# Attention's results stored by halves of the tokens, four heads in a buffer

## The chip, the cores and the metric

The kernel runs on one NeuronCore of one Trainium2 chip. The metric is the device time of one execution in microseconds (us). The kernel before takes 2092.16 us, the median of three runs (2091.04, 2092.16 and 2095.01). The profile is that of one further execution.

## What is computed

One inference step of a two-layer decoder, in fp32, for 512 prompt tokens and 32 sample tokens (8 sequences of 4), 544 columns in all, with 8 heads of 128. Layer A mixes tokens with a gMLP, layer B with a forgetting attention; the keys and values are shared, and the sample also reads pages of a cache. Cut to the part that the change touches:

```python
def fox_prompt(q, k, v, logf):                       # 512 prompt tokens, per block of 128 queries
    s = einsum('bqhd,bkhd->bhqk', qb, k) * scale + cq[..., :, None] - csum[..., None, :]
    p = softmax(where(causal, s, -inf))
    return einsum('bhqk,bkhd->bqhd', p, v)

def fox_sample(q, k_new, v_new, ..., k_past, v_past, ...):   # 32 sample tokens against 256 cached rows each
    p = softmax(concatenate([s_past, s_new]))
    return einsum(p[..., :P], v_past) + einsum(p[..., P:], v_new)

o   = fox_prompt(...) or fox_sample(...)
mix = o.reshape(bsz, L, D_ATT) @ att_w_o[j]          # the projection after attention
h   = h + mix
```

## The kernel before

Activations lie transposed, 128 features on the partitions and the 544 tokens along a row. A product in fp32 is made of three products of a rounded part `hi` and a rest `lo`, so every operand is stored as a pair: ACT writes `hi` with a copy and DVE writes `lo` with a subtraction (L277 and L278, in `split_pair`, for activations and results; L190 and L191, in the weights' own helper; the profile shows these helpers' lines). Nearly all data live in one pool of 44 buffers of 128 x 2 x 544 floats, called `big`. A tile takes a buffer when it is first made and gives it back after its last use.

The attention stage is written as short steps in a list of words (`ORDER`): `f` fetches the keys (`kd`, L974) and values (`vd`, L975) of a head from DRAM, `a` makes the scores and the softmax (L990 to L1012), `t` transposes the weights of a head on TensorE (L1022) and splits them, `v` multiplies by the values (L1040 to L1042) into one PSUM bank `pb` and splits the result into `o[h]`. `s` and `n` make the norm of the queries: its rows go through DRAM and come back by broadcasts (`tmp<-rows`, L711), which DVE multiplies into the queries (L941). `K`, `V` load cache pages (L950, L961), `S`, `T`, `P`, `O` are the sample's attention in two groups of four sequences, of which `O` (L1132, L1133) copies its 16 columns of each head into `o[h]` on POOL. `h` projects columns 0 to 271 in two parts of four heads, `o` projects columns 272 to 543 over all eight heads (L1144 to L1146, added to the residual by DVE at L1156 and L1165).

The order in which the steps are written is not the order on the engines: a list scheduler with its own cost estimates orders the instructions of each engine, and each engine then works strictly in that order, waiting on semaphores. So does SP, which issues all of these loads: a load that has to wait for a free buffer holds up those behind it. The feed-forward stages on both sides have an order written out by hand.

In `o[h]` before, a head has one buffer, with `hi` and `lo` of all its 544 columns:

```python
            o[h] = self.big(F32R)
            self.split_pair(o[h], acc, slice(0, SEQ))
```

Of the kernel before, what the change touches and what calls it, by code (L numbers as in the profile page):

```python
# [22 lines left out]
F32 = mybir.dt.float32  # L23
F32R = mybir.dt.float32r
I32 = mybir.dt.int32
AF = mybir.ActivationFunctionType
ALU = mybir.AluOpType
# [5 lines left out]
SEQ = 512  # L33
NB = 8
NQ = 4
NS = NB * NQ
T = SEQ + NS
HT = T // 2
DFF = 2816
NF = DFF // P  # L40
NH = 8
# [45 lines left out]
class Builder:  # L87
# [876 lines left out]
    def attention(self, xs, acc, h_out, on_chunk):  # L964
        nc = self.nc
        self.fetch_terms()
        q, tile, stat, norm = self.queries(xs, acc)
        o = [None] * NH
        st = {}
        W = (256, 256, 384, 512)  # L970

        def fetch(h):
# [59 lines left out]
        def pv(h):  # L1032
            pt = st.pop(("t", h))
            _, vp = st.pop(("kv", h))
            mv = ((pt[0], 0, 512), (pt[1], 0, 384), (pt[2], 0, 256), (pt[2], 256, 256))
            acc = self.pb()
            for j, (t3, c0, n) in enumerate(mv):
                vs = slice(j * P, (j + 1) * P)
                out = acc[:, 512 - n:512]
                nc.tensor.matmul(out, vp[:, 0, vs], t3[:, 0, c0:c0 + n], start=j == 0, stop=False)  # L1040
                nc.tensor.matmul(out, vp[:, 0, vs], t3[:, 1, c0:c0 + n], start=False, stop=False)
                nc.tensor.matmul(out, vp[:, 1, vs], t3[:, 0, c0:c0 + n], start=False, stop=j == 3)  # L1042
            o[h] = self.big(F32R)
            self.split_pair(o[h], acc, slice(0, SEQ))


        def sample_q():
# [76 lines left out]
            nc.vector.tensor_copy(st["os", g], t[:, :P])  # L1124

        def sample_out(g):
            t = st.pop(("os", g)).rearrange("p (b h t) -> p b h t", h=NH, t=NQ)
            for h in range(NH):
                c0 = SEQ + 16 * g
                hi = o[h][:, 0, c0:c0 + 16].rearrange("p (b t) -> p b t", t=NQ)  # L1130
                lo = o[h][:, 1, c0:c0 + 16].rearrange("p (b t) -> p b t", t=NQ)
                nc.gpsimd.tensor_copy(hi, t[:, :, h, :])  # L1132
                nc.gpsimd.tensor_tensor(lo, t[:, :, h, :], hi.bitcast(F32), ALU.subtract)  # L1133

        def load_vs():
            st["vs"] = self.big()[:, :, :512]
            nc.sync.dma_start(out=st["vs"][:NS], in_=self.vsd[:].rearrange("t (a n) -> t a n", a=2))

        def product(out, hs, w, ks):
            hi, lo = w  # L1140
            for n, k in enumerate(ks):
                c = slice(P * n, P * n + P)
                s, e = n == 0, n == len(ks) - 1
                nc.tensor.matmul(out, hi[:, c], o[k][:, 0, hs], start=s, stop=False)  # L1144
                nc.tensor.matmul(out, hi[:, c], o[k][:, 1, hs], start=False, stop=False)  # L1145
                nc.tensor.matmul(out, lo[:, c], o[k][:, 0, hs], start=False, stop=e)  # L1146

        def project_half(c, part):

            p = self.ps()  # L1150
            hi, lo = self.unit()
            for a in range(2):
                w = slice(4 * P * a, 4 * P * a + 4 * P)
                product(p[:, a, :HT], slice(0, HT), (hi[:, w], lo[:, w]), range(4 * part, 4 * part + 4))
                out = h_out[2 * c + a][:, :HT]
                nc.vector.tensor_tensor(out, p[:, a, :HT], out, ALU.add)  # L1156
                if part == 1:
                    on_chunk(2 * c + a, slice(0, HT))

        def project(c):  # L1160

            p = self.ps()
            product(p[:, 0, :HT], slice(HT, T), self.unit(), range(NH))
            out = h_out[c][:, HT:]
            nc.vector.tensor_tensor(out, p[:, 0, :HT], out, ALU.add)  # L1165
            on_chunk(c, slice(HT, T))

        do = dict(q=tile, s=stat, n=norm, f=fetch, p=prep_q, a=qk, t=turn, v=pv, K=self.load_k, V=self.load_v,
                  z=sample_q, S=sample_qk, T=sample_turn, P=sample_pv, O=sample_out, x=load_vs, h=project_half,
                  o=project)  # L1170
        for step in ORDER.split():
            do[step[0]](*map(int, step[1:]))
# [209 lines left out]
```

## Time and profile before

| | us |
|---|---|
| three runs, median | 2092.16 |
| the profiled execution | 2090.37 |
| its span, first to last instruction | 2088.2 |
| TensorE (PE) busy in the span | 2053.9 |
| VectorE (DVE) | 1521.5 |
| ScalarE (ACT) | 934.8 |
| GpSimd (POOL) | 181.0 |
| attention with its projections, about | 1440 to 1654 of the span |

The profile's rows are read so: start and length in us, the engine, the line of the kernel, the operation, what it writes and reads (names without their numbers), the sizes, how many equal ones follow each other, and in brackets how long the engine had been idle before the first of them and what ended that. The granted TensorE clock was 0.997 of full speed over the span.

### The profile page before, as it was taken

What the parts mean: (1) busy time and instruction counts of PE and PEld (TensorE: products, weight loads), DVE (VectorE), ACT (ScalarE), POOL (GpSimd) and SP (SyncE); (2) the same over time, 40 slices, a digit from 0 to 9 for tenths busy, and PEclk for the clock granted to TensorE, in tenths of its full rate; (3) what the DMA queues carried; (4) which work ended last, traced back from release to release, by engine and by line L of the source; (5) the groups of instructions that cost most, each with busy time, mean ns of one, the idle gap of its engine ahead of it and who ended that gap; (6) DMA issues with size and microseconds to landing.
All of it is one profiled execution on the core that took longest, in us unless ns stands there. A gap on an engine that the chain in (4) does not pass through costs nothing.

```text
span 2088.2 us, 38796 instructions
## 1 busy us (share of the span) xinstructions
PE 2053.9 (98%) x16364; PEld 2016.3 (97%) x16364; DVE 1521.5 (73%) x1893; ACT 934.8 (45%) x1376; POOL 181.0 (9%) x226
## 2 busy tenths in 40 slices
PE   6999999999999999999999999999999999999999
PEld 6999999999999999999999999999977999999999
DVE  7877787556787777776698777786465887777773
ACT  6444344423445344454355344444364654343451
POOL 0000000410100000042050000001041300000020
PEclk9999999999999999999999999999999999999999
DMA  4232324312223232432193322326467322322331
GB/s 163 90 112 73 111 93 140 104 54 71 73 101 117 75 103 81 152 97 81 47 323 148 112 101 91 112 74 198 156 196 267 105 102 72 111 85 98 123 102 44
DMA packets 93776, 237.94 MB, mean 114 GB/s; under 512 B 9490, under 2 KB 27442, under 8 KB 93602
## 3 DMA queue, kind: packets, MB, share of 16 engines
q1 hardware_dynamic: 93458, 235.42, 33.8%
q8 instruction: 129, 2.11, 0.4%
q14 instruction: 45, 0.37, 0.1%
q10 hardware_dynamic: 144, 0.04, 0.0%
HBM read 218.94 MB, written 16.49 MB: 113 GB/s over the span
## 4 chain that ended last, share of the span: by engine, by line
PE 88%; DVE 5%; ACT 3%; DMA 2%; issue 1%; SPq 0%; POOL 0%; ACTq 0%; DVEq 0%; POOLq 0%
PE ps L476 33%; PE ps L233 14%; PE ps L239 14%; PE ps L237 14%; PE pb L476 5%; ACT big L190 1%; DVE big L191 1%; DVE big L176 1%; PE ps L1144 1%; PE ps L1146 1%; PE ps L1145 1%; PE ps L992 0%; PE ps L990 0%; PE ps L1105 0%; DMA big<-in_w13p 0%
## 5 line engine op out<-in xcount | busy, mean ns | idle before, releaser
L476 PE MATMUL ps<-big,big 128*128 128x272 f32 x5760 | 750.2, 289 | 10.6 <-DVE tmp L418 5.3
L476 PEld LDWEIGHTS ps<-big,big 128*128 128x128 f32 x5760 | 735.7, 189 | 12.4 <-ACT tmp L484 6.9
L191 DVE TENSOR_TENSOR big<-big,big 128x1024 fp32r<-128x1024 f32 (+2 forms) x541 | 594.6, 1101 | 107.9 <-ACT big L190 107.7
L190 ACT CAST big<-big 128x1024 fp32r<-128x1024 f32 (+2 forms) x541 | 489.4, 932 | 282.5 <-DVE big L176 275.3
L233 PE MATMUL ps<-big,big 128*128 128x256 f32 x2768 | 576.2, 289 | 12.0 <-ACT big L289 8.8
L239 PE MATMUL ps<-big,big 128*128 128x256 f32 x2768 | 570.9, 288 | 1.0 <-DVE big L191 1.0
L237 PE MATMUL ps<-big,big 128*128 128x256 f32 x2768 | 571.2, 287 | 0.1
L233 PEld LDWEIGHTS ps<-big,big 128*128 128x128 f32 x2768 | 443.5, 189 | 15.4 <-ACT big L289 8.8
L237 PEld LDWEIGHTS ps<-big,big 128*128 128x128 f32 x2768 | 445.9, 189 | 0.6 <-DVE big L290 0.6
L239 PEld LDWEIGHTS ps<-big,big 128*128 128x128 f32 x2768 | 442.8, 188 | 1.8 <-DVE big L191 1.2
L318 POOL TENSOR_TENSOR st<-st,tmp 128x544 f32<-128x544 f32 (+1 forms) x63 | 87.3, 1386 | 1610.9 <-ACT tmp L316 1610.6
L176 DVE TENSOR_TENSOR big<-big,big 128x1024 f32<-128x1024 f32 x160 | 194.9, 1218 | 0.0
L515 DVE SCALAR_TENSOR_TENSOR big<-ps,big 128x544 f32<-128x544 f32 x160 | 115.6, 722 | 106.9 <-PE ps L239 106.7
L484 ACT COPY tmp<-ps 128x544 f32<-128x544 f32 x120 | 73.5, 612 | 146.5 <-PE ps L476 146.2
L476 PE MATMUL pb<-big,big 128*128 128x272 f32 x960 | 127.1, 288 | 0.0
L448 ACT ACTIVATE big<-big 128x544 f32<-128x544 f32 x80 | 52.8, 661 | 161.8 <-DVE big L445 160.0
L476 PEld LDWEIGHTS pb<-big,big 128*128 128x128 f32 x960 | 123.2, 188 | 0.0
L445 DVE TENSOR_TENSOR big<-big,st 128x1088 f32<-128x1088 f32 x80 | 103.2, 1290 | 10.0 <-ACT big L498 8.5
L289 ACT ACTIVATE big<-big,gains 128x544 fp32r<-128x544 f32 (+1 forms) x80 | 55.9, 703 | 118.9 <-DVE big L515 64.9
L278 DVE TENSOR_TENSOR big<-big,big 128x544 fp32r<-128x544 f32 (+1 forms) x96 | 69.5, 724 | 29.0 <-ACT big L277 28.6
L290 DVE SCALAR_TENSOR_TENSOR big<-big,gains,big 128x544 fp32r<-128x544 f32 (+1 forms) x80 | 64.6, 810 | 21.8 <-ACT big L289 21.8
L277 ACT CAST big<-big 128x544 fp32r<-128x544 f32 (+1 forms) x96 | 61.9, 644 | 27.0 <-DVE big L769 15.2
(189 smaller groups left out, 1267.0 us busy)
## 6 DMA issues: line engine op xcount, KB each, us to landing
big<-in_w SPq DMA_DIRECT2D x160, 512.0 KB
big<-in_w2a SPq DMA_DIRECT2D x64, 512.0 KB
big<-in_w2b SPq DMA_DIRECT2D x32, 384.0 KB
big<-in_w13p SPq DMA_DIRECT2D x16, 512.0 KB
big<-in_win SPq DMA_DIRECT2D x16, 512.0 KB
big<-in_wg SPq DMA_DIRECT2D x16, 512.0 KB
big<-in_wkv SPq DMA_DIRECT2D x16, 512.0 KB
big<-in_ck SPq DMA_DIRECT2D x16, 512.0 KB
```

Source lines behind the costliest of these rows:

```text
L176: self.nc.vector.tensor_tensor(t, a, b, ALU.add if op == "+" else ALU.subtract)
L190: self.nc.scalar.copy(hi, src)
L191: self.nc.vector.tensor_tensor(lo, src, hi.bitcast(F32), ALU.subtract)
L233: i = nc.tensor.matmul(out[:, a:b], wh, xh[:, a:b], start=s, stop=False)
L237: nc.tensor.matmul(out[:, a:b], wh, xl[:, a:b], start=False, stop=False)
L239: nc.tensor.matmul(out[:, a:b], wl, xh[:, a:b], start=False, stop=e)
L278: self.nc.vector.tensor_tensor(pair[:, 1, cols], src, pair[:, 0, cols].bitcast(F32), ALU.subtract)
L318: nc.gpsimd.tensor_tensor(acc[:, cols], acc[:, cols], sq, ALU.add)
L445: tt(g, g, rstd.unsqueeze(1).broadcast_to([P, 2, T]), ALU.mult)
L476: nc.tensor.matmul(dst[w], a[:, c], b, start=k in "152" and kp == 0 and n == 0, stop=kp == NKP - 1 and n == 2, skip_group_check=True)
L484: nc.scalar.copy(t["r" + k], t["C" if k == "5" else "A"])
L515: nc.vector.scalar_tensor_tensor(h[c], whole(out), 0.5, h[c], ALU.mult, ALU.add)
```

## The change

Results are kept in eight buffers of another cut. Each holds one half of the tokens (272 columns), one part (`hi` or `lo`) and four heads. The first four are taken when the first head's result is written, the other four when the fifth's is; before, each head took one buffer. The buffers of the first half are given back after the last `h` step, before all eight were kept until the last `o` step. The split after the values' product is made in two pieces of 272 and 240 columns instead of one of 512, and the sample's columns are written by one copy and one subtraction for four heads, where each head had its own two.

```diff
-        o = [None] * NH
-        st = {}
+        st, o = {}, {}
+        def results(half, part, h):
+            k = half, part, h // 4
+            if k not in o:
+                o[k] = self.big(F32R)[:].rearrange("p a (b t) -> p (a b) t", t=HT)
+            return o[k][:, h % 4, :]
...
-            o[h] = self.big(F32R)
-            self.split_pair(o[h], acc, slice(0, SEQ))
+            for half, src in enumerate((acc[:, :HT], acc[:, HT:SEQ])):
+                hi, lo = (results(half, part, h)[:, :src.shape[1]] for part in range(2))
+                nc.scalar.copy(hi, src)
+                nc.vector.tensor_tensor(lo, src, hi.bitcast(F32), ALU.subtract)
...
-            t = st.pop(("os", g)).rearrange("p (b h t) -> p b h t", h=NH, t=NQ)
-            for h in range(NH):
-                c0 = SEQ + 16 * g
-                hi = o[h][:, 0, c0:c0 + 16].rearrange("p (b t) -> p b t", t=NQ)
-                lo = o[h][:, 1, c0:c0 + 16].rearrange("p (b t) -> p b t", t=NQ)
-                nc.gpsimd.tensor_copy(hi, t[:, :, h, :])
-                nc.gpsimd.tensor_tensor(lo, t[:, :, h, :], hi.bitcast(F32), ALU.subtract)
+            t = st.pop(("os", g)).rearrange("p (b h t) -> p h b t", h=NH, t=NQ)
+            c0 = SEQ - HT + 16 * g
+            for k in range(2):
+                hi, lo = (o[1, part, k][:, :, c0:c0 + 16].rearrange("p h (b t) -> p h b t", t=NQ) for part in range(2))
+                nc.gpsimd.tensor_copy(hi, t[:, 4 * k:4 * k + 4])
+                nc.gpsimd.tensor_tensor(lo, t[:, 4 * k:4 * k + 4], hi.bitcast(F32), ALU.subtract)
...
-                nc.tensor.matmul(out, hi[:, c], o[k][:, 0, hs], start=s, stop=False)
-                nc.tensor.matmul(out, hi[:, c], o[k][:, 1, hs], start=False, stop=False)
-                nc.tensor.matmul(out, lo[:, c], o[k][:, 0, hs], start=False, stop=e)
+                xh, xl = (results(half, part, k) for part in range(2))
+                nc.tensor.matmul(out, hi[:, c], xh, start=s, stop=False)
+                nc.tensor.matmul(out, hi[:, c], xl, start=False, stop=False)
+                nc.tensor.matmul(out, lo[:, c], xh, start=False, stop=e)
```

All engines have the same order as before until the attention stage, and again after it. Inside it the scheduler orders them anew. Three places follow, of the kernel before and then of the changed one; the changed kernel's lines lie 6 to 8 further down there (L974 becomes L980, L1022 becomes L1028, L1040 becomes L1046), and its tiles' numbers are up to 3 higher.

SP, in the first third of the stage: `rows` are the norms of the queries of heads 4 to 7, `big2152` and `big2153` the keys and values of head 4, `in_ck` cache pages, with an instruction ahead that sets a register. Before:

```order
L711 DMA tmp2126_17156<-rows2084_16984 128x544
L974 DMA big2152_17265<-kd_10937 128x2x512
L975 DMA big2153_17266<-vd_10938 128x2x512
L711 DMA tmp2147_17236<-rows2084_16984 128x544
L711 DMA tmp2148_17239<-rows2084_16984 128x544
L711 DMA tmp2149_17242<-rows2084_16984 128x544
L950 ISA
L950 DMA big2154_17269<-in_ck 128x8x128
```

Of the changed kernel, where `big2155` and `big2156` are the keys and values of head 4:

```order
L711 DMA tmp2129_17161<-rows2084_16984 128x544
L711 DMA tmp2150_17241<-rows2084_16984 128x544
L711 DMA tmp2151_17244<-rows2084_16984 128x544
L711 DMA tmp2152_17247<-rows2084_16984 128x544
L980 DMA big2155_17270<-kd_10937 128x2x512
L981 DMA big2156_17271<-vd_10938 128x2x512
L950 ISA
L950 DMA big2157_17274<-in_ck 128x8x128
```

The keys and values of head 4 have moved behind three broadcasts. In both kernels the second broadcast waits for TensorE's first transpose of the third head's weights out of the tile that it overwrites, and the next two for the transposes after it.

TensorE, the place of those transposes (into `ps2141`, of the changed kernel `ps2144`) beside the product with the second head's values (into `pb2156`, of the changed kernel `pb2159`). Before:

```order
L1022 MATMUL pb2142_17210<-consts_108,tmp2120_17127 128x128 x2
L1022 MATMUL ps2141_17209<-consts_108,tmp2111_17106 128x128
L1022 MATMUL ps2141_17209<-consts_108,tmp2114_17113 128x128 x2
L1022 MATMUL ps2141_17209<-consts_108,tmp2117_17120 128x128 x2
L1022 MATMUL ps2141_17209<-consts_108,tmp2120_17127 128x128 x2
L1040 MATMUL pb2156_17292<-big2123_17144,big2039_16714 128x512
L1041 MATMUL pb2156_17292<-big2123_17144,big2039_16714 128x512
```

Of the changed kernel:

```order
L1028 MATMUL pb2145_17215<-consts_108,tmp2123_17132 128x128 x2
L1046 MATMUL pb2159_17297<-big2126_17149,big2039_16714 128x512
L1047 MATMUL pb2159_17297<-big2126_17149,big2039_16714 128x512
L1048 MATMUL pb2159_17297<-big2126_17149,big2039_16714 128x512
L1046 MATMUL pb2159_17297<-big2127_17150,big2039_16714 128x384
L1028 MATMUL ps2144_17214<-consts_108,tmp2114_17111 128x128
L1028 MATMUL ps2144_17214<-consts_108,tmp2117_17118 128x128 x2
L1028 MATMUL ps2144_17214<-consts_108,tmp2120_17125 128x128 x2
L1028 MATMUL ps2144_17214<-consts_108,tmp2123_17132 128x128 x2
```

Four of the twelve matmuls of the product now stand ahead of the seven transposes.

POOL, the sample's second group at the end of the stage, between two additions of the norm's squares (L318). Before, with `tmp2327` the sample's results and the other tiles `o[0]`, `o[1]` and so on:

```order
L318 TENSOR_TENSOR st2321_18360<-st2321_18360,tmp2333_18444 128x272
L1132 CAST big2106_17079<-tmp2327_18419 128x16
L1132 CAST big2157_17305<-tmp2327_18419 128x16
L1132 CAST big2159_17321<-tmp2327_18419 128x16
L1132 CAST big2189_17514<-tmp2327_18419 128x16
L1132 CAST big2225_17716<-tmp2327_18419 128x16
L1132 CAST big2237_17803<-tmp2327_18419 128x16
L1132 CAST big2292_18134<-tmp2327_18419 128x16
L1132 CAST big2298_18194<-tmp2327_18419 128x16
L318 TENSOR_TENSOR st2321_18360<-st2321_18360,tmp2335_18463 128x272
L1133 TENSOR_TENSOR big2106_17079<-tmp2327_18419,big2106_17079 128x16
L1133 TENSOR_TENSOR big2157_17305<-tmp2327_18419,big2157_17305 128x16
```

Of the changed kernel, where `big2108` and `big2109` hold `hi` and `lo` of heads 0 to 3 and the other two those of heads 4 to 7:

```order
L318 TENSOR_TENSOR st2321_18376<-st2321_18376,tmp2333_18460 128x272
L1139 CAST big2108_17083<-tmp2327_18435 128x4x16
L1139 CAST big2227_17728<-tmp2327_18435 128x4x16
L318 TENSOR_TENSOR st2321_18376<-st2321_18376,tmp2335_18479 128x272
L1140 TENSOR_TENSOR big2109_17084<-tmp2327_18435,big2108_17083 128x4x16
L1140 TENSOR_TENSOR big2228_17729<-tmp2327_18435,big2227_17728 128x4x16
```

Eight copies have become two, eight subtractions two, and the additions keep their places between them.

More of the change, by code (lines that the diff above doesn't have):

```diff
@@ L1137, in load_vs, with product @@
             nc.sync.dma_start(out=st["vs"][:NS], in_=self.vsd[:].rearrange("t (a n) -> t a n", a=2))
-        def product(out, hs, w, ks):
+        def product(out, half, w, ks):
             hi, lo = w
@@ L1153, in project_half @@
                 w = slice(4 * P * a, 4 * P * a + 4 * P)
-                product(p[:, a, :HT], slice(0, HT), (hi[:, w], lo[:, w]), range(4 * part, 4 * part + 4))
+                product(p[:, a, :HT], 0, (hi[:, w], lo[:, w]), range(4 * part, 4 * part + 4))
                 out = h_out[2 * c + a][:, :HT]
@@ L1162, in project @@
             p = self.ps()
-            product(p[:, 0, :HT], slice(HT, T), self.unit(), range(NH))
+            product(p[:, 0, :HT], 1, self.unit(), range(NH))
             out = h_out[c][:, HT:]
```

## The prediction

> **What bounds the kernel now.** I read the page's table of engines first, then the chain of work that ended last, then the waits of TensorE within the attention stage (1440 to 1660 us), and last the timeline at the three places where the change moves rows.
>
> ```profile
> PE 2053.9 (98%) x16364; PEld 2016.3 (97%) x16364; DVE 1521.5 (73%) x1893; ACT 934.8 (45%) x1376; POOL 181.0 (9%) x226
> PE 88%; DVE 5%; ACT 3%; DMA 2%; issue 1%; SPq 0%; POOL 0%; ACTq 0%; DVEq 0%; POOLq 0%
> ```
>
> TensorE is busy 98% of the span and makes up 88% of the chain. No other engine comes near. So an edit on ACT, DVE or POOL counts only where TensorE waits for it, and the number of matmuls is the same before and after. What TensorE waits for in the stage (us in total, times, longest):
>
> ```profile
> PE ps L1145 <- POOL big L1133: 1.8, 1, 1.8
> PE ps L1144 <- DVE big L1156: 1.5, 2, 0.9
> PE ps L990 <- ACT tmp L1007: 0.7, 1, 0.7
> PE ps L1144 <- POOL big L1132: 0.6, 1, 0.6
> ```
>
> These add up to 1.8 + 1.5 + 0.7 + 0.6 = 4.6 us. That is the ceiling for a gain by removed waits, and 2.4 us of it belong to the sample's columns on POOL. It is 0.22% of the time; 0.2% (4.2 us) is about what a measurement of this kernel can tell from no change.
>
> **The two-piece split: nothing.** A head's result was split by one copy (ACT) and one subtraction (DVE) of 512 columns; now each comes as 272 and 240 columns.
>
> ```profile
> 1590.02 0.38 ACT L277 CAST big<-pb 128x256 fp32r<-128x256 f32 x1
> 1594.38 0.59 ACT L277 CAST big<-pb 128x512 fp32r<-128x512 f32 x1 [2.85 <-PE pb L1042]
> 1590.77 0.41 DVE L278 TENSOR_TENSOR big<-pb,big 128x256 fp32r<-128x256 f32 x1
> 1595.00 0.69 DVE L278 TENSOR_TENSOR big<-pb,big 128x512 fp32r<-128x512 f32 x1 [2.09 <-ACT big L277]
> ```
>
> Two of about 256 columns cost ACT 0.76 in place of 0.59 (+0.17) and DVE 0.82 in place of 0.69 (+0.13). Eight heads make +1.4 and +1.0 us. Both engines sat idle ahead of the long forms (2.85 and 2.09 us), and TensorE's matmuls run beside them; without that cover it would be 2.4 us.
>
> **Term A, the keys of head 4.** SP issues them now behind three broadcasts of norms, of which the second waits for a transpose on TensorE. Before:
>
> ```profile
> 1532.36 0.34 SPq L711 DMA_DIRECT2D tmp<-rows  x1
> 1532.74 0.52 SPq L974 DMA_DIRECT2D big<-kd  x1
> 1533.37 0.56 SPq L975 DMA_DIRECT2D big<-vd  x1
> 1538.82 1.29 SPq L711 DMA_DIRECT2D tmp<-rows  x3
> 1538.40 0.93 PE L1022 MATMUL ps<-consts,tmp 128*128 128x128 f32 x7
> 1539.09 0.48 PE L1040 MATMUL pb<-big,big 128*128 128x512 f32 x1
> 1540.04 0.33 PE L1041 MATMUL pb<-big,big 128*128 128x384 f32 x1
> 1544.40 0.36 PE L992 MATMUL ps<-big,big 128*128 128x256 f32 x1
> ```
>
> The keys were issued at 1532.74 and first used at 1544.40, 11.7 us later. The last of the three broadcasts was issued by 1538.82 + 1.29 = 1540.11. The four matmuls that now stand ahead of the transposes start at 1539.09, and the fifth at 1540.04: 0.95 us. So the broadcasts end at about 1541.06 and the keys follow at about 1541.1, 8.4 us later than before. When do they land?
>
> ```profile
> big<-kd SPq DMA_DIRECT2D x8, 512.0 KB
> tmp<-rows SPq DMA_DIRECT2D x16, 272.0 KB
> 1533.00:1535.50 2.50, 2.50 (x17) 1.91 (x15) 2.24 (x5) 2.38 (x7) 1.88 (x4) 1.00 0.49 128
> 1539.50:1545.00 5.50, 5.49 (x35) 4.62 (x33) 3.89 (x10) 4.54 (x11) 5.19 (x14) 1.00 0.88 176
> 1545.00:1548.00 3.00, 3.00 (x17) 2.27 (x16) 2.15 (x6) 1.08 (x3) 1.01 (x4) 1.00 1.15 337
> 1536.22 0.79 DVE L941 SCALAR_TENSOR_TENSOR big<-big,gains,tmp 128x544 f32<-128x544 f32 x1 [0.17 <-DMA tmp<-rows]
> ```
>
> The windows end with TensorE's granted clock (1.00, full speed), the DMA engines' share and GB/s. Broadcasts move slowly: 128 GB/s where one led the queue (1533.0 to 1535.5), 176 where three did (1539.5 to 1545.0). The queue was at 337 GB/s where pages and keys followed. Three broadcasts are 816 KB, at 176 GB/s 4.6 us. The lone broadcast, issued at 1532.36, released DVE at 1536.22; 272 KB at 128 GB/s are 2.1 us, of which I put 0.8 us ahead of the data and 0.9 behind (an estimate that splits the 1.7 us left). The three's data then run from about 1540.5 to 1545.1, the keys' behind them in 512 / 337 = 1.5 to 1546.6, and TensorE knows of them at about 1547.4.
>
> TensorE arrives at 1544.40 + 0.5 (five transposes, about 0.1 each by the run of seven in 0.69 above, now stand ahead of this matmul; moved, not added) + 0.3 (its share of term B) = 1545.2. The wait is 2.2 us, of which I take **2.1**, since a second chain to the same place, broadcast to DVE's L941 to the split that the transposes of `pb2166` need, costs some 1.4 in the same time and moves the arrival a little. Bounds: 0 if the keys don't stand behind the broadcasts' data (landing by 1545.2), 4.1 at 128 GB/s (816 KB in 6.4 us instead of 4.6, landing at 1549.2). I stay at the middle rate, since its window has just these three broadcasts in it.
>
> What else is queued behind the two moved loads on SP: the pages at L950 go out about 0.95 + 0.52 + 0.56 = 2 us later. Their first user is the second sample group's scores (L1067), more than 100 matmuls on; the next keys behind them have the whole of head 4's turn. Nothing for that.
>
> **Term B, more changes of kind on TensorE.** In the stage's order I count runs of products, transposes (L1022) and 32-row strips (L990, L1105): the changes from one kind to another go from 119 to 132, since the transposes fall into 26 runs instead of 22, the strips L1105 into 6 instead of 4, and L990 into 32 instead of 31.
>
> ```profile
> 1531.78 0.28 PE L1041 MATMUL pb<-big,big 128*128 128x256 f32 x1
> 1531.90 0.28 PE L1042 MATMUL pb<-big,big 128*128 128x256 f32 x1
> 1532.26 0.37 PE L1040 MATMUL pb<-big,big 128*128 128x256 f32 x1
> 1532.47 0.38 PE L1022 MATMUL ps<-consts,tmp 128*128 128x128 f32 x2
> 1532.60 0.36 PE L1041 MATMUL pb<-big,big 128*128 128x256 f32 x1
> 1532.81 0.28 PE L1042 MATMUL pb<-big,big 128*128 128x256 f32 x1
> ```
>
> A matmul of 256 columns hands over after 0.12 us (1531.78 to 1531.90). With a transpose behind it, it takes 0.21 (1532.26 to 1532.47), and behind the transposes 0.21 again (1532.60 to 1532.81), while the two transposes between hand over in 0.13, less than the 0.2 of two in the run of seven. So a visit costs between 0.09 + 0.09 − 0.07 = 0.11 and 0.18 for two changes. 13 changes cost 0.7 to 1.2; as some fall where TensorE waits anyway, I take **+0.8** and bounds 0.3 to 1.3.
>
> **Term C, the sample's columns at the end.**
>
> ```profile
> 1624.00 1.07 POOL L318 TENSOR_TENSOR st<-st,tmp 128x272 f32<-128x272 f32 x1 [4.14 <-ACT tmp L316]
> 1625.03 2.43 POOL L1132 CAST big<-tmp 128x16 fp32r<-128x16 f32 x8
> 1627.41 0.75 POOL L318 TENSOR_TENSOR st<-st,tmp 128x272 f32<-128x272 f32 x1
> 1628.13 3.62 POOL L1133 TENSOR_TENSOR big<-tmp,big 128x16 fp32r<-128x16 f32 x8
> 1628.60 0.39 PE L1145 MATMUL ps<-big,big 128*128 128x272 f32 x1 [1.81 <-POOL big L1133]
> 1621.85 1.22 DVE L191 TENSOR_TENSOR big<-big,big 128x1024 fp32r<-128x1024 f32 x1
> ```
>
> TensorE continues at 1628.60 when the first subtraction is done. Ahead of it stand an addition, eight copies of 0.30 and another addition of 0.75. Of the changed kernel there are two copies and one subtraction, each of 64 columns, an operation that the trace doesn't show. By the nearest rows a copy lies between 0.30 (16 columns) and four times that (1.2), a subtraction between 0.45 and 1.8. An addition of 272 columns takes only 0.75, so most of the price is per instruction; I take 0.4 and 0.5. Then: 1625.03 + 2 x 0.4 + 0.75 + 0.5 = 1627.1, which is 1.5 sooner. DVE's order has one more split of a weight (L191, 1.22 as in the last row) ahead of the sample's last steps now; I let it take back only 0.1, since TensorE's wait at this place names POOL. **−1.4**, bounds −1.8 (the whole wait) and, at four times the price, 1625.03 + 2.4 + 0.75 + 1.8 = 1630.0, **+1.4**. What is late next is L1156 on DVE, whose 0.9 us of wait stays.
>
> **Sum:** +2.1 + 0.8 − 1.4 = **+1.5 us**, 2091.9 against the profiled execution's 2090.37. That execution lies 1.8 below the median of 2092.16, within the runs' own spread, so against the median it is 2093.7.
>
> **Rivals.**
>
> 1. *The keys land in time.* [...] For it: the values of an earlier head moved at twice the rate of the broadcasts beside them.
>
> ```profile
> 1494.10 0.55 SPq L975 DMA_DIRECT2D big<-vd  x1
> 1494.74 1.49 SPq L711 DMA_DIRECT2D tmp<-rows  x3
> 1495.50:1497.50 2.00, 2.00 (x18) 2.00 (x17) 0.00 (x0) 0.00 (x0) 0.00 (x0) 1.00 0.93 302
> 1497.50:1499.50 2.00, 2.00 (x18) 2.00 (x18) 0.23 (x1) 0.00 (x0) 0.00 (x0) 1.00 0.52 146
> ```
>
> Against it: there the rate fell from 302 to 146 GB/s when the values were through, as in a queue that works in order. [...] Time: 0.8 − 1.4 = −0.6, 2091.6. Chance 0.22.
>
> 2. *The end doesn't get faster.* If DVE's added split delays the sample's results by its whole 1.2 us, POOL's shorter list starts later by as much and is worth 1.5 − 1.2 = 0.3: the sum is +2.1 + 0.8 − 0.3 = +2.6, 2094.8. DVE's part in TensorE's waits there (1.5 us at L1156) speaks for it; the 2.4 us that name POOL, and POOL's own 4.14 us idle before the addition, released by ACT and not by DVE, speak against. Chance 0.12.
>
> 3. *Slower: the keys share the lanes with what follows them.* If the keys' 512 KB finish only together with the values and two cache pages (four loads of 512 KB: 128 x 8 x 128 floats are as much), 2048 KB at 337 GB/s take 6.1 us from 1545.1, and 0.9 later, at 1552.1, TensorE goes on: a wait of 6.9, sum 6.9 + 0.8 − 1.4 = +6.3, 2098.5. It decides where the landing comes after about 1550.0, a wait of 4.8. For it: the loads are issued close together, within 3 us. Against: the order seen in the windows above. Chance 0.13.
>
> 4. *POOL's price goes by elements:* C is +1.4, the sum +4.3, 2096.5, just at the bound of what can be told. Against it is the addition of 272 columns in 0.75. Chance 0.06.
>
> **How the numbers follow.** The forecast, a wait of 0.5 to 4 us ahead of head 4 and a shorter end, has 0.44; its own range is +0.3 to +3.5 us. It, rivals 1 and 2 and two thirds of rival 4 are within 0.2%: 0.44 + 0.22 + 0.12 + 0.04 = 0.82. Slower by over 0.2%: rival 3 and a third of rival 4, 0.15. Faster by over 0.2% needs more than nine tenths of the 4.6 us of waits, which no case here gives; 0.03 is left for it. The range goes from rival 1 with C at its best, 2092.16 + 0.8 − 1.8 = 2091.2, less 0.7 for the runs' spread, to nearly rival 3's: 2090.5 to 2098.0.
>
> **What would show it.** Term A: TensorE idle ahead of head 4's first product (L998 of the changed kernel), released by the keys' DMA, 1 to 3 us, and SP's row of the keys near 1541. Idle released by DVE's split there instead means the second chain. No idle is rival 1, over 4.8 us is rival 3. Term C: the wait of 1.8 for POOL near 1628 falls under 0.5, and POOL's four long operations take 0.4 to 0.5 each. Term B: the same stretches of matmuls, with no idle between, some 0.8 longer over the stage. The forecast is wrong if the attention stage as a whole changes by more than 4 us, or if the feed-forward stages, whose orders are the same, change by more than a few tenths.

## The result, and the profile after

The changed kernel takes 2098.62 us (median of 9 runs, 2095.96 to 2100.6); the kernel before took 2092.3 in the same comparison (9 runs). The ratio is 1.0029, with an interval of 1.0020 to 1.0038: slower by some 6 us, where 1.5 had been forecast with a range up to 2098.0. The profiled execution took 2100.6 us, the longest of the nine; the profiled execution of the kernel before, 2090.37, lies near the low end of its runs. So the spans of the two traces lie 10.6 us apart, more than the medians.

The page after, its first rows and the chain:

```profile
span 2098.8 us, 38794 instructions
PE 2061.3 (98%) x16364; PEld 2021.4 (96%) x16364; DVE 1521.8 (73%) x1901; ACT 936.1 (45%) x1384; POOL 177.4 (8%) x202
PE 88%; DVE 5%; ACT 3%; DMA 2%; issue 1%; POOL 1%; SPq 0%; ACTq 0%; DVEq 0%; POOLq 0%
```

The number of matmuls is the same, yet TensorE is busy 2061.3 us instead of 2053.9. So the matmuls themselves took 7.4 us longer. That is not what a wait looks like: a wait would lengthen the span and leave the busy time alone. The waits of TensorE in the attention stage (us in total, times, longest) are these:

```profile
PE pb L1028 <- DVE big L1052: 1.8, 1, 1.8
PE ps L1152 <- DVE big L1164: 1.1, 2, 1.0
PE ps L998 <- DMA big<-kd: 1.1, 1, 1.1
PE ps L1153 <- POOL big L1140: 0.9, 1, 0.9
PE ps L996 <- ACT tmp L1013: 0.9, 2, 0.7
PE ps L1152 <- POOL big L1139: 0.6, 1, 0.6
PE ps L1028 <- ACT tmp L1013: 0.4, 1, 0.4
```

They add up to 6.8 us, 2.2 more than the 4.6 of before. The first and the third stand ahead of head 4, where the prediction put its term A. TensorE's timeline there:

```profile
1546.01 0.44 PE L1028 MATMUL ps<-consts,tmp 128*128 128x128 f32 x2
1548.28 0.52 PE L1028 MATMUL pb<-consts,tmp 128*128 128x128 f32 x3 [1.83 <-DVE big L1052]
1549.91 0.58 PE L998 MATMUL ps<-big,big 128*128 128x256 f32 x1 [1.11 <-DMA big<-kd]
1550.29 0.41 PE L999 MATMUL ps<-big,big 128*128 128x256 f32 x1
1550.50 0.41 PE L1000 MATMUL ps<-big,big 128*128 128x256 f32 x1
```

Two waits, 1.83 + 1.11 = 2.94 us, with three transposes between. Behind them a matmul of 256 columns hands over after 0.21 us (1550.29 to 1550.50); before, it was 0.12. The windows say why; their last three columns are the granted TensorE clock, the DMA engines' share and GB/s:

```profile
1545.87:1549.28 3.41, 1.10 (x6) 0.51 (x5) 2.32 (x6) 1.17 (x4) 3.41 (x18) 1.00 0.96 327
1549.28:1552.69 3.41, 2.78 (x10) 2.33 (x11) 0.86 (x2) 1.00 (x3) 0.22 (x1) 0.50 1.15 324
1552.69:1556.11 3.42, 3.42 (x10) 2.32 (x9) 2.26 (x7) 1.82 (x6) 0.00 (x0) 0.50 1.02 348
1556.11:1559.52 3.41, 3.41 (x62) 2.90 (x64) 1.49 (x5) 1.45 (x4) 2.15 (x2) 0.50 1.15 327
1559.52:1562.93 3.41, 3.41 (x83) 3.08 (x76) 1.08 (x4) 1.73 (x3) 0.00 (x0) 1.00 1.05 379
...
1634.61:1638.02 3.41, 1.87 (x13) 1.44 (x12) 2.07 (x4) 2.07 (x5) 3.41 (x6) 1.00 0.59 195
1638.02:1641.43 3.41, 3.41 (x17) 3.41 (x17) 2.94 (x2) 1.87 (x2) 3.25 (x3) 0.50 0.29 118
1641.43:1644.84 3.41, 3.41 (x29) 3.41 (x28) 1.84 (x3) 1.68 (x3) 0.94 (x2) 1.00 0.33 101
```

TensorE worked only 1.10 us of the 3.41 from 1545.87 on. From 1549.28 the clock was granted at half speed for three stretches of 3.41 us, 10.2 us in all. In the attention stage it happened once more, at 1638.02, for one stretch, behind one in which TensorE had worked 1.87 us. (The windows begin and end where the clock changes; the second fall lies 26 x 3.413 us behind the first.)

What the profiled execution lost, then: +2.2 us of waits; at half clock, by an estimate that takes work at a clock of 0.50 as half done, (10.2 − 0.6 idle) / 2 = 4.8 and 3.4 / 2 = 1.7. That is 8.7 of the 2098.8 − 2088.2 = 10.6 us. Of the rest, 0.9 lies ahead of the stage, as its first score matmul shows, before and after:

```profile
1506.93 0.38 PE L990 MATMUL ps<-big,big 32*128 32x256 f32 x1
```

```profile
1507.82 0.38 PE L996 MATMUL ps<-big,big 32*128 32x256 f32 x1
```

Ahead of the stage TensorE waited 1.0 us longer for DVE's L418 (one wait of 1.68 where it was 0.64). Of the remaining 1.0, 0.4 lies behind the stage, whose last L1153 starts at 1662.28 (before, its last L1145 at 1652.11), and 0.6 in it, somewhat less than the prediction's term B.

The kernel before knows the half clock too, in a place that the prediction didn't look at. Its windows at the end of the attention stage, and behind it in the feed-forward stage (the changed kernel has its like there from 1696.05, and each of the two traces has two more stretches at 0.50, from 43.34 before and from 44.02 after):

```profile
1627.12:1630.53 3.41, 1.93 (x15) 1.93 (x16) 2.73 (x3) 3.41 (x5) 3.41 (x9) 1.00 0.50 159
1681.73:1685.14 3.41, 1.41 (x12) 1.20 (x10) 3.11 (x5) 3.05 (x4) 0.00 (x0) 1.00 0.31 70
1685.14:1688.55 3.41, 3.41 (x15) 3.41 (x16) 2.30 (x3) 1.41 (x2) 0.00 (x0) 0.50 0.21 84
1688.55:1691.96 3.41, 3.41 (x29) 3.41 (x28) 2.24 (x3) 1.44 (x3) 0.00 (x0) 1.00 0.28 92
```

Of the stretches shown, the one in which TensorE worked 1.93 us was followed by full clock, those with 1.10, 1.41 and 1.87 us by half clock.

### The profile page after: what moved, and what is told of

The parts are those of the page before. It is cut to its first block, busy times and chain, and to the rows that moved or that the text cites. A ratio compares the mean times of both kernels' runs of the same rounds, so it can differ in the third digit from the quotient of the medians.

```text
span 2098.8 us, 38794 instructions
## 1 busy us (share of the span) xinstructions
PE 2061.3 (98%) x16364; PEld 2021.4 (96%) x16364; DVE 1521.8 (73%) x1901; ACT 936.1 (45%) x1384; POOL 177.4 (8%) x202
## 4 chain that ended last, share of the span: by engine, by line
PE 88%; DVE 5%; ACT 3%; DMA 2%; issue 1%; POOL 1%; SPq 0%; ACTq 0%; DVEq 0%; POOLq 0%
PE ps L476 33%; PE ps L233 14%; PE ps L239 14%; PE ps L237 14%; PE pb L476 5%; ACT big L190 1%; DVE big L191 1%; DVE big L176 1%; PE ps L1152 1%; PE ps L1153 1%; PE ps L1154 1%; PE ps L998 1%; PE ps L996 0%; PE pb L1075 0%; PE ps L1113 0%
## 5 line engine op out<-in xcount | busy, mean ns | idle before, releaser
L476 PE MATMUL ps<-big,big 128*128 128x272 f32 x5760 | 750.0, 289 | 10.7 <-ACT tmp L484 5.5
L476 PEld LDWEIGHTS ps<-big,big 128*128 128x128 f32 x5760 | 735.6, 189 | 12.5 <-ACT tmp L484 7.0
L318 POOL TENSOR_TENSOR st<-st,tmp 128x544 f32<-128x544 f32 (+1 forms) x63 | 88.5, 1405 | 1616.7 <-ACT tmp L316 1616.4
L476 PE MATMUL pb<-big,big 128*128 128x272 f32 x960 | 127.1, 288 | 0.0
L476 PEld LDWEIGHTS pb<-big,big 128*128 128x128 f32 x960 | 123.2, 188 | 0.0
```

Source lines behind the costliest of these rows:

```text
L318: nc.gpsimd.tensor_tensor(acc[:, cols], acc[:, cols], sq, ALU.add)
L476: nc.tensor.matmul(dst[w], a[:, c], b, start=k in "152" and kp == 0 and n == 0, stop=kp == NKP - 1 and n == 2, skip_group_check=True)
```

## The experiments

Three theories stood beside each other. **C:** head 4's keys behind the broadcasts make TensorE wait, and the wait makes the granted clock fall, which costs more than the wait. **W:** only the waits count; the fall of the clock is something else that happened to lie there. **L:** the layout itself (more pieces, more changes of kind) costs all over the stage.

The table has the median of each kernel, its ratio, with the interval, to the kernel before run beside it (the row of before is that of runs 5 to 8; beside runs 1 to 4 it had 2092.25, beside 9 and 10 2091.92), and two numbers that I work out from every run: the time lost to the clock, span x (1 − mean granted clock), and the mean time less that. The clock is given to three decimals, so one run's loss is good to about 1 us, and the formula counts idle TensorE at half clock too; the means are rough to about half a us.

| kernel | runs | median us | ratio (interval) | lost to the clock | mean less that |
|---|---|---|---|---|---|
| before | 35 | 2092.03 | | 7.2 | 2085.6 |
| changed | 9 | 2098.62 | 1.0029 (1.0020 to 1.0038) | 10.7 | 2088.1 |
| 1 long filler | 10 | 2097.15 | 1.0020 (1.0010 to 1.0029) | 5.7 | 2091.5 |
| 2 keys behind, old layout | 12 | 2097.22 | 1.0014 (1.0002 to 1.0025) | 10.8 | 2085.8 |
| 3 keys ahead | 12 | 2091.94 | 1.0004 (0.9994 to 1.0013) | 7.5 | 2085.4 |
| 4 keys and split ahead | 12 | 2091.22 | 0.9996 (0.9988 to 1.0005) | 6.4 | 2085.5 |
| 5 short filler | 12 | 2094.16 | 1.0009 (0.9998 to 1.0020) | 7.2 | 2088.3 |
| 6 split ahead, keys behind | 12 | 2098.26 | 1.0022 (1.0012 to 1.0033) | 10.1 | 2088.0 |
| 7 two pieces, old layout | 12 | 2092.24 | 0.9997 (0.9987 to 1.0006) | 6.4 | 2085.6 |
| 8 keys ahead, tail | 12 | 2089.89 | 0.9985 (0.9975 to 0.9994) | 5.4 | 2084.9 |
| 9 keys ahead, 16 operations | 11 | 2093.25 | 1.0007 (0.9998 to 1.0016) | 7.0 | 2086.4 |
| 10 tail, old layout | 11 | 2088.84 | 0.9988 (0.9979 to 0.9997) | 6.6 | 2083.5 |

**Runs 1 and 5: the wait filled with work.** By theory C the clock should not fall if TensorE is kept busy while it would wait, though head 4 begins no sooner. In the changed kernel, ahead of head 4's first product:

```diff
+                for _ in range(24 if (h, i) == (4, 0) else 0):
+                    nc.tensor.matmul(out[:, :P], self.identr, self.neg[:, :P], start=False, stop=False)
                 nc.tensor.matmul(out[:, :w], qp[:, 0, qs], kp[:, 0, :w], start=False, stop=False)
```

The columns of `neg` that it reads are zeros, so nothing is added to the scores. Run 1 had 48 of them.

> The changed kernel with 48 matmuls of 128 columns that add zeros to head 4's first score tile; 24 of them stand right around the transposes at which TensorE waits, 24 a little earlier. They add work of about 48 x 0.055 = 2.7 us, nearly as much as the 2.9 us that TensorE waits there. Theory C (the clock: TensorE idle for 2.9 us ahead of head 4 makes the granted clock fall to half for 10 us, which costs 5 us beside the wait): the waits at this place fall below 0.6 us, head 4's matmuls still begin near 1549.9, the granted clock stays at 1.00 between 1548 and 1560, and the time falls by about 5 us, to 2093.5. Rival W (the fall of the clock has nothing to do with this wait, only the waits themselves count): the clock falls to 0.5 all the same and the time stays at 2098.6 or above. Rival L (the layout costs all over the stage): 2098.6 or above, the clock may be either.

Measured: 2097.15, so the time of theory C, 2093.5, was missed. No wait was left at this place, the clock stayed at 1.00, but a filler took 0.115 us and not 0.055, so that head 4 began later than in the changed kernel's trace: by 1.0 us, or by 1.5 counted from the stage's first score matmul. In the table it lost 5.0 us less to the clock than the changed kernel, and took 3.4 us more of everything else, more than that 1.5; where the rest lies the run doesn't show. I had mis-sized the filler, and took half as many.

> The filler of the first run was too long: its matmuls took 0.115 us each there, 48 of them 5.5 us, more than the wait of 2.9, and head 4 began 1.0 us later on the trace. Here 24 of them, 2.75 us, all a little ahead of the wait. Theory C: head 4 begins where it does in the changed kernel (near 1549.9), the waits there are below 0.5 us, the clock stays at 1.00, and the time is 4 to 5 us below that of the changed kernel: 2093.5 to 2094.8. Rival W: 2098.6 or above, with the clock at 0.5 behind 1549.

Measured: 2094.16. The stage's first score matmul, the first product of head 4 and the windows of run 5:

```profile
1506.94 0.38 PE L996 MATMUL ps<-big,big 32*128 32x256 f32 x1
1549.15 0.39 PE L1000 MATMUL ps<-big,big 128*128 128x256 f32 x1 [0.57 <-DMA big<-kd]
```

```profile
1545.00:1550.00 5.00, 4.43 (x30) 3.64 (x28) 4.27 (x9) 2.17 (x7) 4.12 (x18) 1.00 1.00 320
1550.00:1560.00 10.00, 10.00 (x164) 8.60 (x163) 5.99 (x17) 5.86 (x15) 2.15 (x2) 1.00 1.09 332
```

Head 4 begins 42.2 us behind the stage's first score matmul, as in the changed kernel (42.1). The clock is 1.00 where the changed kernel had 0.50, and the kernel with *more* work is 4.5 us faster than the changed one by the medians (the intervals of the two ratios touch at 1.0020). Nine of its 12 executions took 2093.3 to 2095.2 us with mean clocks of 0.997 to 0.999, three took 2098.5 to 2102.2 with 0.993 to 0.995; of the changed kernel's nine, eight took 2098.2 or more with 0.994 or 0.995. Less its loss to the clock it takes what the changed kernel takes (2088.3 and 2088.1): the delay ahead of head 4 is still there, only the fall of the clock is gone. W falls.

**Run 2: the order of SP alone, in the old layout.** A dependency without data holds the two loads behind the last broadcast:

```diff
-                nc.sync.dma_start(out=t, in_=rows[j].partition_broadcast(P))
+                self.bc = nc.sync.dma_start(out=t, in_=rows[j].partition_broadcast(P)).ins
...
+            with self.tc.issue_after(self.bc) if h == 4 else ExitStack():
                 nc.sync.dma_start(out=kp[:, :, :SEQ].bitcast(F32), in_=self.kd[h])
                 nc.sync.dma_start(out=vp[:, :, :SEQ].bitcast(F32), in_=self.vd[h])
```

> The kernel before, with its own layout, in which only the loads of head 4's keys and values are put behind the three broadcasts of norms. Theory C: the last broadcast is issued by 1540.1 as before, the keys land 7.4 us behind it as in the changed kernel, near 1547.6, TensorE arrives at 1544.6, waits some 3 us for the keys' DMA in one piece, the clock falls to half for one to three stretches of 3.4 us, and the time is 5 to 8 us longer: 2097 to 2100. Rival W: +3 us, 2095.3, clock 1.00. Rival L: no change, 2092.3.

Measured: 2097.22, 5.0 us over the kernel before beside it, with a wide spread (2091.0 to 2101.7). Its waits and windows:

```profile
PE ps L992 <- DMA big<-kd: 3.0, 1, 3.0
```

```profile
1550.00:1560.00 10.00, 10.00 (x144) 8.14 (x145) 3.49 (x13) 3.84 (x12) 2.15 (x2) 0.67 1.06 340
```

The wait is of the size expected, 3.0 us for the keys, and the clock falls behind it. So the order of two loads makes most of the slowdown without any new layout. In the table nearly all of it is loss to the clock; why the mean less that is hardly above the kernel before's, where a wait of 3 us should show, the runs don't settle.

**Runs 3 and 4: the new layout, its keys ahead.** In the list of steps `f4` is named seven steps earlier; run 4 also holds DVE's multiplications of three norms behind the second head's split.

```diff
-t1 n4 a3 t2 p4 n5 n7 n6 z f4 K5 v1 v2 f5 p5 K6 t3 a4 S0 v3 f6 h00 p6 V5 f7 a5 K7 t4 K4 v4 t5 p7 V7
+t1 n4 f4 a3 t2 p4 n5 n7 n6 z K5 v1 v2 f5 p5 K6 t3 a4 S0 v3 f6 h00 p6 V5 f7 a5 K7 t4 K4 v4 t5 p7 V7
```

> The changed kernel, with the fetch of head 4 named earlier in the list of steps, so that its keys and values are issued ahead of the three broadcasts again; nothing else is edited, and DVE's second piece of the split still stands behind two multiplications that need the broadcasts. Theory C: no wait for the keys; TensorE still waits 1.5 to 2 us for DVE ahead of the transposes into pb. [...] Rival W: 2098.6 - 1.1 = 2097.5. Rival L: 2098.6.

> As the run before, and DVE's multiplications of the norms of heads 5 to 7 stand behind both pieces of the second head's split, so that nothing at this place waits for a broadcast. Theory C: no wait of TensorE over 0.3 us ahead of head 4, clock 1.00 there, and with 2.9 us of waits and 5 us of half clock gone 2090.5 to 2092, no slower than the kernel before. Rival W: 2098.6 - 2.9 = 2095.7. Rival L: 2096 to 2098.6.

Measured: 2091.94 and 2091.22, both not to be told from the kernel before. In run 3 the wait for DVE, which I had expected to stay, went as well: with the keys there, the scheduler also put head 4's first products ahead of the transposes that had waited for DVE. All the waits over 0.2 us that are left in its stage:

```profile
PE ps L1152 <- DVE big L1164: 1.1, 2, 1.0
PE ps L1153 <- POOL big L1140: 0.9, 1, 0.9
PE ps L996 <- ACT tmp L1013: 0.9, 2, 0.7
PE ps L1152 <- POOL big L1139: 0.6, 1, 0.6
```

L falls: the whole new layout stands in run 3, and the loss is gone with the place of two loads.

**Run 6: which of the two waits sets the end.** The changed kernel with its late keys, and only DVE's order as in run 4 (`v1` ahead of `n5` in the list, and):

```diff
-            with self.tc.issue_after(box["last"].ins):
+            with self.tc.issue_after(self.split_end if h in (5, 6, 7) else box["last"].ins):
```

> The changed kernel, with its keys late, in which only DVE's multiplications of the norms of heads 5 to 7 stand behind both pieces of the second head's split. If the keys' landing sets where TensorE goes on (theory C), the wait for DVE goes and that for the keys' DMA grows to 2.7 to 3.1 us, in one piece, and the time is as that of the changed kernel, 2097.5 to 2100. If DVE's chain sets it, the wait in all falls to 1.1 us, the clock doesn't fall, and the time is below 2093.5.

Measured: 2098.26. The two waits became one, of about the length of both:

```profile
PE ps L998 <- DMA big<-kd: 3.2, 1, 3.2
```

So the landing of the keys sets where TensorE goes on; the wait for DVE was only in front of it.

**Run 7: the two pieces alone,** in the old layout.

```diff
-            self.split_pair(o[h], acc, slice(0, SEQ))
+            for c0, c1 in ((0, 272), (272, 512)):
+                self.split_pair(o[h], acc[:, c0:c1], slice(c0, c1))
```

> The kernel before, with its own buffers, in which only the split of a head's result is made in two pieces of 272 and 240 columns: 8 more instructions each on ACT and DVE. The keys of head 4 stay ahead of the broadcasts. Theory C: no wait over 0.3 us ahead of head 4, 2091.8 to 2092.8. Rival L (the pieces themselves cost): over 2094.

Measured: 2092.24, no difference, as expected.

**Runs 8 to 10: the end of the stage.** POOL's list there in the changed kernel:

```profile
1633.32 1.02 POOL L318 TENSOR_TENSOR st<-st,tmp 128x272 f32<-128x272 f32 x1 [6.93 <-ACT tmp L316]
1634.28 1.65 POOL L1139 CAST big<-tmp 128x64 fp32r<-128x64 f32 x2
1635.89 0.75 POOL L318 TENSOR_TENSOR st<-st,tmp 128x272 f32<-128x272 f32 x1
1636.61 0.84 POOL L1140 TENSOR_TENSOR big<-tmp,big 128x64 fp32r<-128x64 f32 x2
```

Two additions of the norm's squares, which nobody waits for yet, stand ahead of what TensorE waits for. Run 8 is run 3 with `O0 O1` ahead of `h11` in the list and

```diff
                 if part == 1:
-                    on_chunk(2 * c + a, slice(0, HT))
+                    with self.tc.issue_after(self.out_end) if c else ExitStack():
+                        on_chunk(2 * c + a, slice(0, HT))
```

where `out_end` is POOL's last subtraction of the group.

> The changed kernel with the keys of head 4 ahead (as in the third run) and, at the end of the stage, POOL's copies and subtractions of the sample's second group ahead of the additions L318, which wait behind them. If POOL's list sets TensorE's waits of 0.6 and 0.9 us there, these two go, less than 0.3 stays of them, and the clock falls less often behind them: 2089.5 to 2091, faster than the kernel before. If DVE's backlog sets them, they come back under DVE's name, and the time stays at 2092.

Measured: 2089.89, faster than the kernel before (ratio 0.9985, 0.9975 to 0.9994). Of POOL's waits this is left:

```profile
PE ps L1153 <- POOL big L1140: 0.3, 1, 0.3
```

Run 9 is run 3 with the sample's columns written head by head again, 16 POOL operations for a group:

> The changed kernel with the keys of head 4 ahead (as in the third run), and the sample's columns written head by head again, 16 POOL operations a group instead of 4, into the new buffers. If POOL's price is mostly per instruction, as the traces of before and of the changed kernel read, the second wait for POOL at the end of the stage goes back from 0.9 to about 1.8 us, and the time is 0.5 to 1.5 us above the third run's 2091.9. If it goes by elements, the wait stays at 0.9 and the time at 2091.9.

Measured: 2093.25, 1.3 above run 3, and the wait is back at its old length:

```profile
PE ps L1153 <- POOL big L1140: 1.8, 1, 1.8
```

So the four-head operations are worth about 0.9 us of waiting here (the intervals of runs 3 and 9 overlap; the wait shows it). Run 10 takes the edit of run 8 at the end of the stage (without the keys) to the old layout, with its 16 operations:

> The kernel before, in its own layout, with POOL's copies and subtractions of the sample's second group ahead of the additions L318 at the end of the stage. If the order of POOL's list is what the eighth run gained by, the waits of 0.6 and 1.8 us for POOL fall to 1.2 or less together, and the time is 1 to 2 us below that of the kernel before: 2090 to 2091. If the gain needs the four-head operations, the waits stay above 2 us and the time at 2092.

Measured: 2088.84, the fastest of all (ratio 0.9988, 0.9979 to 0.9997) and below the 2090 to 2091 expected. Its waits for POOL went from 2.4 to 0.7 us, and the table's last column falls by 2.1:

```profile
PE ps L1145 <- POOL big L1133: 0.7, 1, 0.7
```

So the order of POOL's list gains by itself, and the new layout isn't needed for it; the intervals of runs 8 and 10 overlap. Both beat the kernel before and the changed one.

## Why the prediction was wrong

The step that failed is the sum. It counted each wait as worth its own length, +2.1 us for term A, and left out, without a reason, what a wait does to the granted clock behind it. Run 5 shows that price with the end of the wait where it was: 4.5 us between the medians, 3.5 by the means of what was lost to the clock. The wait itself is the smaller part: run 3, without it, takes 2.7 us less than the changed kernel besides the clock. No rival had the clock either: rival 3, the slower one, asked for a wait of 6.9 us and put its own decision at 4.8, and 2.9 were enough; that its 2098.5 is nearly the measured time is luck. The sign of being wrong that the prediction had set, a change of over 4 us in the stage, came: from its first score matmul to its last L1153 it took 154.5 us, against 145.2 before. The page's row of the clock in 40 slices reads 9 throughout; the half clock of before at 1685 would have been seen only in windows of a few us.

Point by point:

- **Term A** had the right place and mechanism (run 2 alone, run 3 without it), and was too small: 2.1 forecast, 2.94 measured. SP's rows after:

```profile
1533.25 9.14 SPq L711 DMA_DIRECT2D tmp<-rows  x4
1542.43 0.53 SPq L980 DMA_DIRECT2D big<-kd  x1
```

  The keys went out at 1542.43, not 1541.1, and TensorE knew of them 7.4 us later, at 1549.9; I had 6.3 and 1547.4. The upper bound of 1549.2 was short too. The window from which I had taken 176 GB/s moved 176 x 5.5 = 968 KB, more than the 816 of the three broadcasts, so it wasn't theirs alone; where the 1.1 us more from issue to landing lie, the runs don't show. The keys' later issue has a reason: I had moved the broadcasts by the four matmuls alone; the chain of waits of the changed kernel leads from ACT's exponentials over POOL's scaling of the weights (L1016), which ends at 1542.24, to the last broadcast.
- **The second chain** over DVE was named, and sized at 1.4 with no working shown; it took 1.83. It didn't add to the keys' wait (run 6). The three broadcasts that DVE waits for landed late:

```profile
1544.49 0.78 DVE L941 SCALAR_TENSOR_TENSOR big<-big,gains,tmp 128x544 f32<-128x544 f32 x1 [0.27 <-DMA tmp<-rows]
1547.03 0.79 DVE L941 SCALAR_TENSOR_TENSOR big<-big,gains,tmp 128x544 f32<-128x544 f32 x1 [1.09 <-DMA tmp<-rows]
1547.73 0.40 DVE L1052 TENSOR_TENSOR big<-pb,big 128x240 fp32r<-128x240 f32 x1
```

- **Rival 1** falls: the keys did not come in time. TensorE waited 1.11 us for their DMA in the changed kernel's trace and 3.0 in run 2's.
- **Term B,** +0.8: about right in size, as far as it can be read. Run 3 has the new layout, no wait ahead of head 4 and no half clock in its stage; its waits add up to 3.7 us (with one of 0.2 not shown) against 4.6 before, and yet its stage is as long as before: 145.2 us from the first score matmul (1507.58, before 1506.93) to the last L1153 of the projection (1652.78, before L1145 at 1652.11). So 0.9 went into the work between; that it is all changes of kind isn't shown.
- **Term C,** −1.4: −0.9 measured (1.8 to 0.9; run 9 takes it back). The subtraction took 0.42, forecast 0.5; the copy of 64 columns 0.82 where I had taken 0.4. What was missing is the copies' price. Rival 2's late start isn't seen: POOL's list began when ACT released it, as before, and the gain of 0.9 is above that rival's 0.3. Rival 4 doesn't hold either, though the copy cost as much as 2.7 of the small ones, at 0.30.
- **The split in two pieces,** nothing: right (run 7).
- **The stages on both sides:** in the profiled execution 0.9 us longer ahead of attention and 0.4 behind it. In the other profiles of kernels with the same order ahead, the first score matmul lies between 1506.93 and 1507.71, so most of the 0.9 needs no change of the kernel.

## What to carry to other kernels

Where TensorE is the bound, as here with 98% of the span, a wait of 2 to 3 us need not be paid by its length alone: behind the changed kernel's 2.94 us the clock stood at 0.50 for 10.2 us, and run 2, with a wait of 3.0, was 5.0 us slower. So read the granted clock in windows of a few us behind every wait, in the kernel before as well, and price a new wait with the half clock that may follow. A load that a scheduler moves behind others that wait is a change of its own, whatever the edit was about (run 2), and naming its step earlier may undo it, as in run 3 (2091.94 where the changed kernel took 2098.62). An engine's list in front of what the bound engine waits for is worth reading through for work that nobody waits for yet: here that was worth 2.1 us in run 10's mean less its loss to the clock.

## What the runs showed of the hardware

**The clock.** The half clock came in pieces of one (at 1638.02, and at 1685.14 before), two (near 45 us), three (at 1549.28) and five stretches of 3.41 us. Five, 17.1 us, were in run 10's profiled execution, and there the fall came behind a stretch with only 0.70 us of idle:

```profile
1520.33:1523.74 3.41, 2.71 (x14) 1.90 (x15) 2.67 (x8) 2.01 (x7) 2.17 (x2) 1.00 0.02 5
1523.74:1527.15 3.41, 3.41 (x9) 2.35 (x9) 1.25 (x4) 1.25 (x4) 0.00 (x0) 0.50 0.01 3
...
1537.39:1540.80 3.41, 3.41 (x15) 3.22 (x15) 1.38 (x4) 0.67 (x2) 1.64 (x2) 0.50 0.00 0
1540.80:1544.22 3.42, 3.42 (x21) 2.51 (x21) 2.05 (x6) 2.69 (x8) 1.01 (x3) 1.00 0.63 217
```

TensorE's records fill these five stretches (3.41 us of each), and the clock stayed at half all the same; in a row of products of 272 columns (L476) it came back after one (1685.14 above). What sets run 10's place apart in the trace is its mix of transposes, strips of 32 rows and short runs of products. That this mix is the cause was not tried. Whether the work in a stretch decides, and how much of it, the traces don't settle: the clock fell behind stretches with 1.87 us of work out of 3.41 in the changed kernel and 2.71 in run 10, and stayed at 1.00 behind one with 1.93 in the kernel before. The longest gap ahead of the fall at 1549.28 was 1.83 us; the next, 1.11 us, ended at 1549.91, behind it.

In the changed kernel's trace the falls at 1549.28, 1638.02 and 1696.05 lie whole numbers of stretches apart, 26 and 17. The clock also differs between executions of one kernel: the 35 runs of the kernel before went from 2090.26 to 2099.52 us, with mean clocks from 0.998 down to 0.993, 0.005 x 2090 = 10 us apart. Which waits the clock fell behind in each of them isn't shown.

**POOL beside DVE.** In the changed kernel a copy of 64 columns took 0.82 us beside DVE's split of a weight, which itself took 1.79 where the split at 1631.11, with POOL idle, took 1.23; in run 3, for the sample's first group, with DVE idle beside them, two copies took 0.41 together:

```profile
1633.62 1.79 DVE L191 TENSOR_TENSOR big<-big,big 128x1024 fp32r<-128x1024 f32 x1
```

```profile
1615.72 0.41 POOL L1139 CAST big<-tmp 128x64 fp32r<-128x64 f32 x2 [24.74 <-DVE tmp L1132]
```

So of one size a copy took 0.82 us beside DVE's split and about 0.2 with DVE idle. That DVE is the cause was not tried.
